# HGRN heads' four projections as two pairs, with half of the weight sums made by adding DMAs, and small work moved between engines

## The chip, the cores and the metric

The kernel runs on one core of one Trainium2 chip. The core has five engines that run side by side, each through its own queue in a fixed order: TensorE (PE in the profile; its weight loads are PEld), VectorE (DVE), ScalarE (ACT), GpSimd (POOL), and SyncE (SP), which here issues almost all DMAs. The metric is the time of one execution on the device in microseconds; lower is better. The traces are profiled executions of the same program.

## The reference

One inference step of a one-layer encoder over T = 32 + 512 tokens: 32 frames of a running stream (the sample) and 512 frames of a new one (the prompt). Everything is float32. After an RMS norm, one large projection `xn @ w_in` (1024 inputs) is cut into the parts of two branches and two gates:

```python
u, v_m, z_m, ig_pre, fg_pre, q_h, f_h, i_h, g_h, ga, gb = jnp.split(proj, _split_points(), axis=-1)
...
lfh = jnp.log(lb + (1.0 - lb) * jax.nn.sigmoid(f_lin))
kh = (1.0 - lb) * jax.nn.sigmoid(-f_lin)
qh = jax.nn.silu(q_h.astype(f32))
oh, S_new = _hgrn(to_heads(qh), to_heads(kh), to_heads(i_h.astype(f32)), to_heads(lfh), S0[l].astype(f32))
oh = _head_rmsnorm(oh.transpose(0, 2, 1, 3), hnorm_g[l].astype(f32)) * jax.nn.silu(g_h.astype(f32))
yb = oh.astype(x.dtype) @ w_brh[l]
y = jax.nn.sigmoid(ga) * ya + jax.nn.sigmoid(gb) * yb
```

The first branch is an mLSTM with four heads of 512 (its output, through `w_brm`, is `ya`). The second, HGRN2, has eight heads of 128: for each head and token, `o = q exp(g) S + sum over earlier tokens of (q, k, decay) v`, with a decay per channel, and the state `S` is carried on. Then come the gated sum, `w_out`, a small per-layer embedding behind a sigmoid gate, and the final norm. Outputs are the tokens and all new states of both streams.

## The kernel before, in words

Tokens lie along the free dimension, channels on the 128 partitions. To keep float32 accuracy, TensorE multiplies in a reduced format: each operand is split in a high part (a cast on ScalarE) and a low part (a subtraction on VectorE), and each product is three matmuls, high by high, high by low and low by high. A projection of 128 output channels is a *unit*; its weights come as two raw pieces of 128 x 512 by a DMA on SP (`raw_piece`, L118) and are split by `split_piece` (high L128, low L129).

There are two ways to make units. `One` (matmuls L366) computes one unit as eight input blocks x three products x two token halves = 48 matmuls. `Two` computes two units with seven instead of eight half-size products (Winograd's form of Strassen's method): the token sums are made once (`xf`), the weight sums s1 to s4 in `make` (VectorE, L418), each of seven blocks is 12 matmuls of 272 columns (L453), and `after1` to `after7` evict the partial products: some are kept in SBUF by ScalarE (L467), some added to or subtracted from a kept one by VectorE (L474, L476), one is negated by ScalarE (L478). With w = [[a0, a1], [b0, b1]] for units a and b and their two pieces, s1 = b0 + b1, s2 = s1 + a0, s3 = a0 + b0 and s4 = s2 + a1.

`Pump` puts the blocks of a list of units in one order (two neighbouring pairs overlap in it), loads raw pieces up to four ahead (RAWAHEAD), prepares weights three blocks ahead (AHEAD), and hands out the matmuls in steps of six. A chain of other work is a generator: each `yield n` lets the pump run n steps, and then the chain issues its own matmuls. TensorE's order is therefore written out by hand; on the other engines a scheduler fixes an order when the program is built, and SP and GpSimd too run theirs in that order. A semaphore wait holds everything behind it on its engine.

Stages: the opening (norm, first projections, gate rows); four mLSTM heads, each with a pump; then one pump for `units()`: per HGRN head h the single units f, q, i, g, and after them eight pairs of the two merge gates ga and gb. Beside that pump runs `chain(h)` for one HGRN head after another: seven levels of decay (chunk lengths 1 to 64). In each level ScalarE copies the far keys (km, L1390), TensorE makes the products pl (L1398; the sample's at L1406), VectorE multiplies keys hk and queries hq by the decay (L1416), multiplies decays with each other (L1420) and picks the level's entries into `at` under a mask (L1421, sample L1423). After the first level the diagonal terms q*k are transposed (pd) and summed (dg). Then the triangles `aa` are cut out of `at` on GpSimd with the constant `tri` (L1446, L1452), values and keys are transposed (ht), state products are made (su, L1474), the chunk states follow one from the other in VectorE (tile tf, L1477, L1479), and the outputs (ho, L1497 to L1501) read `aa`, `at` and the chunk states. The diagonal is added (L1506, L1507), and the norm follows (L1512 to L1522). `finish(h)` transposes the head's output two or three levels into the next head's chain and multiplies it by the gate.

The pump also evicts the single units of a head: `forget` makes tf and hk (sigmoids on ScalarE, scaling on VectorE, L1324 to L1329), `query` makes q, hq and kq (L1335 to L1340, kq on GpSimd), `value` copies, `gate` makes silu as x * sigmoid(x). After the chains come the rest of the gate pairs, then `w_brh`, `w_out` and the last gate.

In the opening, four value units are projected; the copy of the fourth out of PSUM (`values_out`, L1222) is called in the part where only TensorE's order is written by hand. PSUM tiles of projections share four banks (pool `pd`).

Of the kernel before, what the change touches and what calls it, by code (L numbers as in the profile page):

```python
# [14 lines left out]
ALU = mybir.AluOpType  # L15

P = 128
# [24 lines left out]
NSUM = 4  # L42
# [20 lines left out]
def hybrid_step(ctx: ExitStack, tc: tile.TileContext, a, o):  # L63
# [228 lines left out]
    tri = cp.tile([P, 2, P], F32, name="tri")  # L292
    pick(tri[:, 0, :], ALU.is_gt, 0, 1, -1, 1.0, 0.0)
    pick(tri[:, 1, :], ALU.is_gt, 0, -1, 1, 1.0, 0.0)
    sxt = cp.tile([P, P], F32, name="sxt")
# [32 lines left out]
    xf = [None] * (KD // 2)  # L328

    class One:  # L330
# [9 lines left out]
        def blocks(self, first):  # L340

            return [
                (i, [(self.unit, i // 2)] if i % 2 == 0 else [], self.prepare(i // 2) if i % 2 == 0 else None, self.run(i), {})
                for i in range(3)
            ] + [(3, [], None, self.run(3), {self.key: 1})]

        length = 4
# [35 lines left out]
    class Two:  # L383
# [3 lines left out]
        length = 7  # L387

        def __init__(self, what, f, unit, dest, then):
            self.what, self.f, self.unit, self.dest, self.then = what, f, unit, dest, then  # L390
            self.sums, self.w, self.t, self.late = {}, {}, {}, None

        def raws(self):
            a, b = self.unit, self.unit + 1
            return [(a, 0), (b, 0), (b, 1), (a, 1)]

        def blocks(self, first):
            a, b = self.unit, self.unit + 1
            times = (0, 3, 1, 6, 5, 9, 11) if first else (0, 3, 5, 6, 8, 9, 11)
            k = (self.what, self.f), (self.what, self.f + 1)  # L400
            return [
                (times[0], [(a, 0)], self.make("a11"), self.run("a11", 0, True, self.after1), {}),
                (times[1], [(b, 0), (b, 1)], self.make("s2"), self.run("s2", 0, False, self.after6), {}),
                (times[2], [(a, 1)], self.make("a12"), self.run("a12", 1, True, self.after2), {}),
                (times[3], [], self.make("s3"), self.run("s3", 0, False, self.after7), {}),
                (times[4], [], self.make("s1"), self.run("s1", 1, True, self.after5), {}),
# [3 lines left out]

        def make(self, form):
            def go(raw):
                a, b = self.unit, self.unit + 1
                q = self.sums

                def add(name, x, y):
# [1326 lines left out]
```

## Time and profile before

| | |
|---|---|
| median of 3 runs | 1174.36 us (1173.25 to 1174.53) |
| the profiled execution | 1174.53 us, its span 1172.8 us |
| busy: TensorE / VectorE / ScalarE / GpSimd | 1160.9 / 883.9 / 614.9 / 143.5 us |
| granted TensorE clock | 0.999 |
| DMA | 135.82 MB, mean 116 GB/s |
| DMA queues | SP's and ScalarE's hardware queues; no DMA is issued from GpSimd |
| one HGRN head (752.68 to 788.34 us) | 35.66 us |

Times are in us from the span's start unless marked ns. In a row of instruction groups stand line, engine, operation, output <- input with shapes, the count, then busy us and mean ns of one, and last the engine's idle time just before them and what ended it. A row of a stretch gives the busy time (and count) of PE, PEld, DVE, ACT and POOL, the granted clock, the share of the DMA engines and GB/s. A row of the chain of waits is the start, the length and the piece that the end of the program waited for. Matmuls overlap, so a row's mean is longer than the step from one to the next.

### The profile page before, as it was taken

What the parts mean: (1) busy time and instruction counts of PE and PEld (TensorE: products, weight loads), DVE (VectorE), ACT (ScalarE), POOL (GpSimd) and SP (SyncE); (2) the same over time, 40 slices, a digit from 0 to 9 for tenths busy, and PEclk for the clock granted to TensorE, in tenths of its full rate; (3) what the DMA queues carried; (4) which work ended last, traced back from release to release, by engine and by line L of the source; (5) the groups of instructions that cost most, each with busy time, mean ns of one, the idle gap of its engine ahead of it and who ended that gap; (6) DMA issues with size and microseconds to landing.
All of it is one profiled execution on the core that took longest, in us unless ns stands there. A gap on an engine that the chain in (4) does not pass through costs nothing.

```text
span 1172.8 us, 24295 instructions
## 1 busy us (share of the span) xinstructions
PE 1160.9 (99%) x9089; PEld 1130.5 (96%) x9089; DVE 883.9 (75%) x2156; ACT 614.9 (52%) x1357; POOL 143.5 (12%) x283
## 2 busy tenths in 40 slices
PE   9999999999999999999999999999999999999998
PEld 8989999999999999999999999999999999999998
DVE  6977988686996768967885677877788998654485
ACT  5676557654665556665572343343434666433462
POOL 4933011110111000210000101111101100000000
PEclk9999999999999999999999999999999999999999
DMA  6124215232353233542637222212122273332753
GB/s 231 63 94 128 91 46 175 93 109 100 122 179 115 82 118 117 173 138 93 219 102 238 64 70 62 70 62 71 55 70 63 76 242 99 106 100 77 236 170 113
DMA packets 77902, 135.82 MB, mean 116 GB/s; under 512 B 8788, under 2 KB 16340, under 8 KB 77784
## 3 DMA queue, kind: packets, MB, share of 16 engines
q1 hardware_dynamic: 77616, 134.21, 35.4%
q8 instruction: 71, 1.16, 0.4%
q14 instruction: 47, 0.39, 0.1%
q10 hardware_dynamic: 168, 0.06, 0.0%
HBM read 109.32 MB, written 24.91 MB: 114 GB/s over the span
## 4 chain that ended last, share of the span: by engine, by line
PE 86%; DVE 3%; ACT 1%; issue 1%; ACTq 0%; DVEq 0%
PE d L453 22%; PE d L366 18%; PE ya L149 8%; PE pg L1602 4%; PE yb L149 4%; PE o L149 4%; PE C L833 4%; PE q L149 3%; PE k L149 3%; PE pl L1398 2%; PE nm L1003 2%; PE sc L793 2%; PE ple L149 1%; PE nm L980 1%; PE ht L1464 1%
## 5 line engine op out<-in xcount | busy, mean ns | idle before, releaser
L1390 ACT COPY km<-hk 128x256 f32<-128x256 f32 x56 | 24.0, 429 | 82.0 <-DVE hk L1416 60.0
L569 DVE SCALAR_TENSOR_TENSOR cv<-ub,vec,cv 128x547 f32<-128x547 f32 x48 | 40.3, 840 | 1.3 <-ACT cv L564 0.7
L1398 PE MATMUL pl<-hq,km 128*128 128x128 f32 x224 | 36.0, 284 | 0.0
L1416 DVE TENSOR_TENSOR hq<-hq,q 128x128 f32<-128x128 f32 (+1 forms) x96 | 25.3, 293 | 9.5 <-PE pl L1398 8.3
L933 DVE SCALAR_TENSOR_TENSOR c<-c,wi,Cs 128x258 f32<-128x258 f32 x32 | 15.3, 477 | 21.8 <-PE Cs L931 21.8
L1398 PEld LDWEIGHTS pl<-hq,km 128*128 128x128 f32 x224 | 30.8, 190 | 0.0
L467 ACT COPY t<-d 128x272 f32<-128x272 f32 x78 | 29.6, 379 | 1.2 <-PE d L453 1.0
L1452 POOL TENSOR_TENSOR at<-at,tri 32x32 f32<-32x32 f32 x8 | 4.0, 496 | 208.5 <-DVE at L1423 208.5
L1071 DVE TENSOR_TENSOR y<-ya,y 128x272 f32<-128x272 f32 x48 | 18.9, 434 | 10.7 <-PE ya L149 10.1
L1416 DVE TENSOR_TENSOR hk<-hk,q 128x128 f32<-128x128 f32 x96 | 26.1, 285 | 0.3 <-ACT km L1390 0.2
L845 ACT COPY Co<-C 128x258 f32<-128x258 f32 x32 | 10.4, 378 | 29.2 <-PE C L833 24.7
L1421 DVE COPY_PREDICATED at<-lmask,pl 128x256 f32<-128x256 uint8 x56 | 24.7, 441 | 0.0
L1512 ACT ACTIVATE osq<-kq 128x128 f32<-128x128 f32 x32 | 9.9, 311 | 25.8 <-DVE kq L1506 25.1
L1340 POOL TENSOR_TENSOR kq<-q,hk 128x544 f32<-128x544 f32 x8 | 13.9, 1742 | 61.3 <-DVE q L1338 58.4
L1014 ACT COPY y<-nm 128x516 f32<-128x516 f32 x16 | 9.4, 590 | 21.7 <-PE nm L1003 21.7
L562 POOL COPY uo<-ub 128x3 f32<-128x3 f32 x16 | 11.5, 717 | 71.2 <-DVE ub L474 50.0
L833 PE MATMUL C<-vh,kwl 128*128 128x258 f32 x96 | 19.4, 283 | 0.0
L833 PE MATMUL C<-vl,kwh 128*128 128x258 f32 x96 | 19.4, 283 | 0.0
L833 PE MATMUL C<-vh,kwh 128*128 128x258 f32 x96 | 19.4, 283 | 0.0
L963 DVE BATCH_NORM_STATS2 bs<-y 128x6 f32<-128x512 f32 (+1 forms) x20 | 13.8, 691 | 6.4 <-ACT y L1014 6.2
L731 POOL COPY vsm<-vt 128x96 f32<-128x96 f32 x16 | 7.0, 446 | 87.1 <-ACT vt L478 44.0
L807 ACT CAST sh<-dm 128x512 fp32r<-128x512 f32 (+3 forms) x16 | 7.4, 460 | 18.9 <-DVE dm L801 17.4
(4086 smaller groups left out, 4880.1 us busy)
## 6 DMA issues: line engine op xcount, KB each, us to landing
ya_d<-y SPq DMA_DIRECT2D x32, 272.0 KB, 2.1
y<-ya_d SPq DMA_DIRECT2D x24, 272.0 KB, 4.3
c<-in_C SPq DMA_DIRECT2D x16, 258.0 KB, 3.5
out_Cp<-Co SPq DMA_DIRECT2D x16, 258.0 KB, 2.6
out_Cs<-c SPq DMA_DIRECT2D x16, 258.0 KB, 2.3
x<-in_xT SPq DMA_DIRECT2D x8, 272.5 KB, 4.8
ya<-ya_d SPq DMA_DIRECT2D x8, 272.0 KB, 4.3
h<-in_xT SPq DMA_DIRECT2D x8, 272.0 KB, 3.7
```

The lines of the kernel that those rows point to most:

```text
L149: PE.matmul(both[b][:m, :TH], part(w, off + k * step, m, x), xx[:, half(b)], start=(k == 0 and j == 0), stop=(k == n - 1 and j == 2),)
L366: PE.matmul(self.ps[b][:, : c.stop - c.start], part(self.w, k * P, P, x), xx[:, c], start=(k == 0 and j == 0), stop=(k == KD - 1 and j == 2),)
L453: PE.matmul(ps, ww[:, c], xx, start=(start and k == 0 and j == 0), stop=end, skip_group_check=not start,)
L467: S.copy(t, ps)
L569: V.scalar_tensor_tensor(cv[:, :547], ub[:, j : j + 547], vcol(V_CW + 4 * ft + j), cv[:, :547], ALU.mult, ALU.add)
L793: PE.matmul(pn[:, 0, :n], ks[f][x][:, j * P : (j + 1) * P], qs[f][y][:, NS + j * P : T], start=(f == 0 and i == 0), stop=(f == KH - 1 and ...
L833: PE.matmul(pn[g][:, :VH], kw[b][x][:, f * P : (f + 1) * P], vv[b][y][:, g * VH : (g + 1) * VH], start=(b == 0 and j == 0), stop=(b == NB ...
L1390: S.copy(km.rearrange("p (n j c) -> p n j c", j=2, c=c), view(kk, HB, ((2 * c, NA // (2 * c)), (c - HB, 2), (1, c))),)
L1398: PE.matmul(pn[:, 0, b * P : (b + 1) * P], km[:, b * P : (b + 1) * P], view(qq, b * P, ((2 * c, P // (2 * c)), (HB + c, 2), (1, c))), star ...
L1416: V.tensor_tensor(xv[:, :, i, :], xv[:, :, i, :], t[:, :, 1 - i : 2 - i].to_broadcast([P, m, c]), ALU.mult)
L1421: V.copy_predicated(at[:, :NA], lmask[:, li, :NA], pn[:, 0, :NA])
L1602: PE.matmul(ps, part(w, k * P, P, x), xx[:, c], start=(k == 0 and j == 0), stop=(k == KD - 1 and j == 2))
```

## The change

Projections of an HGRN head become two pairs: units q and f, and units g and i. `One` remains for four z units of the first mLSTM head. Per pair, the sums s1 and s3 come from DMAs: SP loads b0 into two buffers, and a DMA issued on GpSimd's queue adds b1 to the one and a0 to the other while it loads them; s2 and s4 stay on VectorE. The raw piece b0 is no longer loaded by itself. The pump begins these three blocks ahead of the pair's first block in the order of preparation (LEAD). The eight pairs of the merge gates do the same. s4 is now added in place in the buffer of s2, and the ring of sum buffers has five instead of four.

```diff
-NSUM = 4
+NSUM = 5
+LEAD = 3
...
+        def begin(self):
+            a, b = self.unit, self.other
+            for name, u, i in (("s1", b, 1), ("s3", a, 0)):
+                t = self.sum_tile(name)
+                nc.sync.dma_start(t, w_in[b][:, :WP])
+                G.dma_start(t, w_in[u][:, i * WP : (i + 1) * WP], accum_op=ALU.add)
...
                 if form == "s2":
-                    add("s1", raw[b, 0], raw[b, 1])
-                    add("s2", q["s1"], raw[a, 0])
-                if form == "s3":
-                    add("s3", raw[a, 0], raw[b, 0])
+                    if not self.early:
+                        add(self.sum_tile("s1"), raw[b, 0], raw[b, 1])
+                    add(self.sum_tile("s2"), q["s1"], raw[a, 0])
+                if form == "s3" and not self.early:
+                    add(self.sum_tile("s3"), raw[a, 0], raw[b, 0])
...
+                while self.begins and self.begins[0][0] <= self.made:
+                    self.begins.pop(0)[1].begin()
```

The eviction follows: a pair's results land in SBUF tiles (the value unit through reversed slices, `value_tile`), and ScalarE and VectorE work from there. The scalings of tf and hk move to ScalarE, silu is one ScalarE operation (so silu and sigmoid alternate there), and kq moves from GpSimd to VectorE:

```diff
-            V.tensor_scalar(tf[:, :T], tf[:, :T], lcc, lbc, ALU.mult, ALU.add)
-            V.tensor_scalar(kk[:, :T], kk[:, :T], lcc, None, ALU.mult)
+            S.activation(tf[:, :T], tf[:, :T], AF.Identity, scale=lcc, bias=lbc)
+            S.mul(kk[:, :T], kk[:, :T], lcc)
...
-            V.tensor_tensor(unrev(q0), acc[0][:, :HB], unrev(q0), ALU.mult)
-            V.tensor_tensor(q0[:, HB:T], acc[1][:, :NA], q0[:, HB:T], ALU.mult)
+            S.activation(unrev(q0), qq[:, :HB], AF.Silu)
+            S.activation(q0[:, HB:T], qq[:, HB:T], AF.Silu)
             V.tensor_tensor(qq[:, :T], q0[:, :T], tf[:, :T], ALU.mult)
-            G.tensor_tensor(kq[:, :T], q0[:, :T], kk[:, :T], ALU.mult)
+            V.tensor_tensor(kq[:, :T], q0[:, :T], kk[:, :T], ALU.mult)
```

In the chain the sample's product gets 128 instead of 32 weight columns, so one mask operation serves both parts, and one operation multiplies both sides' decays from the second level on; the diagonal sums come from one reduction; the triangles are cut by GpSimd's select without the constant `tri`; the diagonal terms are made by ScalarE ahead of the outputs, which VectorE then adds; one state copy and the norm's last products move to ScalarE; `finish` comes one level later.

```diff
-                PE.matmul(pn[:NS, 0, NA:HB], kk[:, csmp], qq[:, csmp], start=True, stop=True)
+                PE.matmul(pn[:, 0, NA:HB], kk[:, NA : NA + P], qq[:, csmp], start=True, stop=True)
...
-            V.copy_predicated(at[:, :NA], lmask[:, li, :NA], pn[:, 0, :NA])
-            if smp:
-                V.copy_predicated(at[:NS, NA:HB], lmask[:NS, li, NA:HB], pn[:NS, 0, NA:HB])
+            V.copy_predicated(at[:, :n], lmask[:, li, :n], pn[:, 0, :n])
...
-            if li == 2 and h:
+            if li == 3 and h:
...
-            G.tensor_tensor(
-                aa[:, j],
-                at[:, :NA].rearrange("p (b t) -> p b t", b=2),
-                tri[:, j : j + 1, :].to_broadcast([P, 2, P]),
-                ALU.mult,
-            )
+            for b in range(2):
+                triangle(aa[:, j, b], at[:, b * P : (b + 1) * P], 1 - 2 * j)
...
+                for b in range(NB):
+                    S.mul(ov[:, b * P : (b + 1) * P], it[:, b * P : (b + 1) * P], dg[:, b : b + 1])
...
-        V.tensor_copy(sb[:, :P], pu[:, 0, :P])
+        S.copy(sb[:, :P], pu[:, 0, :P])
...
-            V.scalar_tensor_tensor(ov[:, d], it[:, d], dg[:, b : b + 1], po[:, 0, d], ALU.mult, ALU.add)
+        V.tensor_tensor(ov[:, :NP], po[:, 0, :], ov[:, :NP], ALU.add)
...
+        for b in range(NB):
+            S.mul(ov[:, b * P : (b + 1) * P], ov[:, b * P : (b + 1) * P], hr[:, b : b + 1])
```

Two smaller moves: the new sample state `sn` shares its two buffers with the loaded one (`s0`), and the mask input `sxt` a buffer of the small pool. In the opening, the last `values_out()` is called ahead of the gate rows, in the part where ScalarE's order too is written by hand:

```diff
         st8[0]["wk"] = weight(a["w_km"][0, 0], "wk00", eng=G)
+        values_out()
         for _ in range(GATED):
             next(gates)
```

209 lines of the change are left out of this document (116 added, 93 removed).

## Prediction

> **What bounds the kernel now.** I read first the page's busy times and the shares of the chain that ended last, then the busy times by stage, then the chain of waits inside one HGRN head, and last the rows of VectorE, ScalarE, GpSimd and the DMA queue there. The page, its head and a line of its fourth part:
>
> ```profile
> span 1172.8 us, 24295 instructions
> ...
> PE 1160.9 (99%) x9089; PEld 1130.5 (96%) x9089; DVE 883.9 (75%) x2156; ACT 614.9 (52%) x1357; POOL 143.5 (12%) x283
> ...
> PE d L453 22%; PE d L366 18%; PE ya L149 8%; PE pg L1602 4%; PE yb L149 4%; PE o L149 4%; PE C L833 4%; PE q L149 3%; PE k L149 3%; PE pl L1398 2%; PE nm L1003 2%; PE sc L793 2%; PE ple L149 1%; PE nm L980 1%; PE ht L1464 1%
> ```
>
> TensorE sets the time, and the single projections (L366) and the paired ones (L453) are its largest parts. By stage, one window in which the last head runs beside paired projections, and one whole head beside single ones (columns: engine busy us, TensorE clock, DMA share, GB/s):
>
> ```profile
> 894.00:927.00 33.00, 32.97 (x253) 30.60 (x253) 31.09 (x89) 14.79 (x34) 3.25 (x3) 1.00 0.14 43
> 752.68:788.34 35.66, 35.66 (x279) 33.71 (x279) 27.04 (x99) 14.05 (x39) 4.04 (x5) 1.00 0.21 65
> ```
>
> A head takes 35.66 us and TensorE has no gap in it; VectorE is busy 27.04 us and ScalarE 14.05 us. The chain of waits through that head, and the longest piece of paired projections after the heads:
>
> ```profile
> 773.03 0.45 PE pl L1398 x4
> ...
> 780.57 0.44 PE ho L1497 x4
> ...
> 781.91 0.22 PE ho L1499 x2
> ...
> 788.17 0.18 PE pl L1406 x2
> ...
> 939.02 54.37 PE d L453 x431
> ```
>
> Every link is TensorE. A 272-column matmul costs 54.37/431 = 0.126 us at the margin. Two times matter below, counted from the last level's product at 773.03: the outputs (ho) come 7.5 us later, and the last read of a chunk state 8.9 us.
>
> **The change, part by part.**
>
> *Pairs instead of singles.* Two single projections are 2 x 48 = 96 matmuls, a pair 7 x 12 = 84. Sixteen pairs remove 192 matmuls: 192 x 0.126 = 24.2 us, all on the path. The other insertions of a head stay, so its pitch would fall by 3.0 us to 32.6 us. 28 pump steps a head now equal the 28 that a chain consumes (27 without the finish), so chain follows chain; work after the last head shrinks from 92 to 84 steps of 6 matmuls.
>
> *Wider sample weights.* The 40 sample products now load 128 weight columns instead of 32. Two passes took 0.18 us, and four 128-wide ones 0.45 us, thus 0.09 against 0.11 each: 0 to 40 x 0.04 = 1.6 us. I take 0.8.
>
> *VectorE.* Rows of the head, and of the window after it where they exist only there:
>
> ```profile
> L1339 DVE TENSOR_TENSOR hq<-q,tf 128x544 f32<-128x544 f32 x1 | 1.9, 1897 | 0.0
> L1420 DVE TENSOR_TENSOR q<-q 128x4 f32<-128x4 f32 (+9 forms) x12 | 1.5, 177 | 0.0
> L1506 DVE SCALAR_TENSOR_TENSOR kq<-hi,dg,ho 128x128 f32<-128x128 f32 x4 | 1.1, 340 | 0.0
> L1423 DVE COPY_PREDICATED at<-lmask,pl 32x32 f32<-32x32 uint8 x5 | 0.9, 173 | 0.0
> L1354 DVE TENSOR_TENSOR hg<-d,hg 128x272 f32<-128x272 f32 x2 | 0.8, 432 | 0.0
> L1516 DVE TENSOR_TENSOR kq<-kq,hr 128x512 f32<-128x512 f32 x1 | 0.7, 692 | 0.0
> L129 DVE TENSOR_TENSOR wi760l<-wi76r,wi760h 128x512 fp32r<-128x512 f32 x1 | 0.7, 692 | 1.7 <-ACT wi760h L128 1.7
> L1328 DVE TENSOR_SCALAR tf<-tf,lc,lb 128x544 f32<-128x544 f32 x1 | 0.6, 559 | 0.0
> L1329 DVE TENSOR_SCALAR hk<-hk,lc 128x544 f32<-128x544 f32 x1 | 0.5, 499 | 0.0
> L1337 DVE TENSOR_TENSOR q<-d,q 128x288 f32<-128x288 f32 x1 | 0.5, 458 | 2.1 <-ACT q L1335 2.1
> L1338 DVE TENSOR_TENSOR q<-d,q 128x256 f32<-128x256 f32 x1 | 0.4, 414 | 0.0
> ```
> ```profile
> L1361 DVE TENSOR_TENSOR ya<-ya,ga 128x544 f32<-128x544 f32 x2 | 1.4, 725 | 0.0
> L418 DVE TENSOR_TENSOR ws<-ws,wi88r 128x512 f32<-128x512 f32 x2 | 1.4, 688 | 0.0
> ```
>
> Added to a head: 6 more low parts (14 pieces instead of 8) x 0.69 = 4.2; the sums s2 and s4 of two pairs, 4 x 0.69 = 2.8; 6 evictions x 0.43 (the 272-wide row, L1354) = 2.6; kq from GpSimd 0.7: 10.3 us. Removed: the scalings of tf and kk 1.1; the two products with q 0.9; of the gate 0.9; hq falls from 1.9 to about 0.7, since kq no longer runs beside it on GpSimd, 1.2; the output norms 0.7 and their small sample part about 0.3; four diagonal terms and a sample one become two adds, 0.7; the sample masks join the wide ones, 0.7 net; six of the short products of the decay 6 x 0.18 = 1.1; a state copy about 0.3: 7.9 us. VectorE ends at 27.04 + 2.4 = 29.4 us of 32.7, 90%. The first window shows 31.09 of 33.00 us (94%) with TensorE at 32.97 in just such a mix, so I take nothing for load alone. In the branch gates two sums a pair leave VectorE; TensorE is the limit there, and I take nothing.
>
> *ScalarE.* Rows of the head, the page's row of the kept products, and two of the opening:
>
> ```profile
> L128 ACT CAST wi760h<-wi76r 128x512 fp32r<-128x512 f32 x1 | 0.6, 618 | 1.4 <-PE d L366 1.4
> L1512 ACT ACTIVATE osq<-kq 128x128 f32<-128x128 f32 x4 | 1.2, 311 | 2.9 <-DVE kq L1506 2.8
> ```
> ```profile
> L467 ACT COPY t<-d 128x272 f32<-128x272 f32 x78 | 29.6, 379 | 1.2 <-PE d L453 1.0
> ```
> ```profile
> 70.67 1.28 ACT L641 ACT_TABLE_LOAD   x1
> 71.96 0.66 ACT L641 ACTIVATE row<-row 4x544 f32<-4x544 f32 x1
> ```
>
> Added: 6 high parts 3.7; 6 kept and 2 flipped products x 0.38 = 3.0; two 544-wide scalings x 0.66 = 1.3; ten 128-wide products for diagonal and norm x 0.31 = 3.1; a state copy 0.3; two table loads, since silu and sigmoid now alternate, 2 x 1.28 = 2.6. Removed: the value copies and one half of the gate's, 0.9. ScalarE goes to 14.05 + 13.1 = 27.2 us of 32.7, 83%. Its lead of three blocks (three pump blocks are 4.5 us of matmuls) covers the casts; if that cover is gone, a late copy km is late for the next level's product. Page against trace: the Trainium skill, "ScalarE: Activation LUTs", What ACT_TABLE_LOAD costs, adds a drain and puts each switch at about 2.66 us; by that, an estimate, ScalarE would be at 30.0 us and its rival below more likely. The trace does not agree: the activation starts at 71.96, when the 1.28 us are over.
>
> *The adding DMAs.* Per pair two plain loads go to SP's queue and two accumulating ones to GpSimd's; one raw load falls away. Each accumulating one waits on GpSimd for its plain load. Four a head stand in one queue with the triangles and the clearing of at. Rows of the load, of its issue, and of GpSimd:
>
> ```profile
> wi69r<-in_w_in SPq DMA_DIRECT2D x2, 256.0 KB, 2.6
> ```
> ```profile
> 777.96 0.33 SPq L118 DMA_DIRECT2D wi62r<-in_w_in  x1
> ```
> ```profile
> 774.44 1.45 POOL L1446 TENSOR_TENSOR aa<-at,tri 128x256 f32<-128x256 f32 x2 [3.60 <-DVE at L1421]
> L175 POOL TENSOR_SCALAR_AFFINE_SELECT tri<-tri x2: 293/536/778, 3.5 to 4.9; 128x128 f32<-128x128 f32 x2
> ```
>
> In the built order of the changed kernel, in each head, the first accumulating DMA of the next g/i pair stands on GpSimd just ahead of the four triangles, and VectorE's sum s2, which reads its result, stands ahead of the update of the third chunk state. The plain load waits for a buffer that VectorE frees with a low part which I place 0.7 us after the last level's product, behind the products hq and kq. Three issues x 0.4 = 1.2, landing 2.6: 4.5 us after the product. Triangles then take 4 x 0.3 = 1.2 us and are ready before 7.5 unless GpSimd spends over 1.8 us on the DMA. The accumulation from GpSimd's turn to landing is not in the trace: at least the 2.6 us of a plain load, at most about twice that and a GpSimd operation of 1.4 us, 6.6. I take 4.0, nearer to the plain load. Then 4.5 + 4.0 + 0.7 (s2) + 0.3 (update, at the nearest 128-wide row, L1506) = 9.5 against 8.9 us: TensorE waits 0.6 us a head, 8 x 0.6 = 5 us. Bounds: 0 and 8 x 3.2 = 26 us. On SP's queue the next head's sample state now waits, buffers being shared, for ho of the head before, with raw loads behind it; they are issued four pieces ahead of need, more than a pair's 7 blocks of 1.5 us, and I take nothing.
>
> *The opening.* The fourth value copy moves ahead of the gate rows:
>
> ```profile
> 72.94 0.67 PE L149 MATMUL k<-cs0h,wk000h 128*128 128x272 f32 x2 [2.37 <-ACT vt L1222]
> 75.52 0.69 ACT L603 ACTIVATE z<-d 128x272 f32<-128x272 f32 x2
> ```
>
> The wait of 2.37 us ends, but the second k product (due 3 us after the first, at 75.9) needs the banks that z frees at 76.2. ScalarE has the same work ahead of z in either order. The wait moves there: I take 0.3 us of 0 to 2.4.
>
> **Sum**, against the profiled execution of 1174.53 us (span 1172.8 and 1.7 around it; the median of the runs is 1174.36, 0.2 less): 1174.5 - 24.2 + 0.8 - 0.3 + 5 = 1155.8 us.
>
> **Rivals.**
> 1. VectorE or ScalarE becomes the bound of a head through its fixed order. Before, VectorE idles 35.66 - 27.04 = 8.6 us a head; if half of that stays, the pitch is 29.4 + 4.3 = 33.7, or 1.0 us a head over 32.7; with three quarters 3.1. For it: ScalarE doubles. Against it: the 94% window. 8 x 1.0 in place of the 5: 1158.8; at 2 us a head 1167.
> 2. Slower: the accumulation lands late. Each us beyond 3.4 us from GpSimd's turn goes straight into the wait at ho. 24.2 + 0.3 - 0.8 = 23.7 us over 8 heads is 3.0 us a head, so it decides from 6.4 us; at 8 us it is 4.6 x 8 = 37: 1174.5 - 23.7 + 37 = 1187.6. For it: no such DMA is in the trace, and GpSimd and VectorE held each other up (hq 1.90 us beside kq, 0.73 for the same shape elsewhere). Against it: only this one sum of the four a head has so little lead; that of the next q/f pair is read some fifty VectorE instructions after its buffer comes free.
> 3. About the same: VectorE holds up GpSimd while it writes such a DMA's descriptors. Held by one operation of hq's 1.9 us, the landing is 4.0 + 1.9 = 5.9 us, the wait 2.5 us a head or 20 us: 1174.5 - 23.7 + 20 = 1170.8; a second hold on the triangles would close the rest. For it: hq beside kq. Against it: the scalings L1328 and L1329 leave the head. The Trainium skill, "SBUF — State Buffer", SBUF: two separate sides, speaks against the change: descriptors of GpSimd's DMAs cannot be written while VectorE runs a two-port operation, and 0.62 us became 3.1 us there. By that rule this rival is the likely one; hq's row agrees that the two engines block each other, and no run so far has such a DMA.
> That the matmuls do not go is excluded by the built order: 192 fewer.
>
> **How the numbers follow.** Forecast with waits under 1 us a head 0.62 (own range 1148 to 1161); rival 1 0.18 (1159 to 1170); rival 2 0.14; rival 3 0.06, half of it within 0.2% of the time before. No change from no wait at all is 1174.5 - 24.2 - 2.4 = 1148. The range 1147 to 1170 holds the first two. About 0.2% (2.3 us) is what a measurement can tell: faster 0.81, same 0.04, slower 0.15, the last with a little of rival 1's far end.
>
> **What would show it.** Right: pitch between first levels near 33.3 us; paired projections at 0.126 us; a wait at ho of about 0.6 us named for the state tile tf; 30 and 27 us busy on VectorE and ScalarE a head; a software DMA queue whose transfers land 4 us after issue; an early wait that now precedes the second k product. Wrong: TensorE waits at pl for km or hq (rival 1), at ho for aa (GpSimd's queue held the triangles), or for weights of a sum (rival 2), or transfers of more than 6 us.

## The result, and the profile after

The changed kernel takes 1179.01 us (median of 4 runs, 1178.62 to 1181.02), the kernel before 1174.34 us beside it (1173.25 to 1174.53). The ratio is 1.0048, with a 95% interval of 1.0035 to 1.0060: slower by about half a per cent, where 1155.8 us and 1147 to 1170 had been forecast. The profiled execution took 1178.68 us.

The page of the changed kernel, its head, the busy times and the chain that ended last:

```profile
span 1176.7 us, 24263 instructions
PE 1140.0 (97%) x8897; PEld 1110.7 (94%) x8897; DVE 891.7 (76%) x2092; ACT 708.9 (60%) x1565; POOL 181.6 (15%) x335
PE 17%; ACT 1%; DVE 0%; issue 0%; ACTq 0%
```

TensorE has 192 instructions fewer and is busy 20.9 us less, but the span is 3.9 us longer. The chain's 17% for TensorE, after 86% before, says little of where the time went: followed back from the end, it reaches only to 965.50 us, in the merge gates' pairs, and says nothing of the time before. TensorE's waits tell more. Each row names what waited, what ended the wait, and then the us in total, the times and the longest:

```profile
PE pl L1446 <- ACT km L1438: 8.5, 9, 1.1
PE d L467 <- DVE hq L488: 5.3, 1, 5.3
PE d L467 <- ACT t L481: 3.0, 2, 2.1
PE ht L1510 <- DVE hq L1464: 2.6, 6, 0.4
PE k L151 <- ACT z L635: 2.2, 1, 2.2
PE ya L151 <- DVE y L1103: 1.6, 4, 0.4
PE ya L151 <- ACT wbm301h L130: 1.2, 1, 1.2
```

Of these only the wait before k has a counterpart before (2.37 us). The others stand in four places.

**In the heads.** One head after, by the busy times of a stretch (PE, PEld, VectorE, ScalarE, GpSimd, clock, DMA share, GB/s):

```profile
740.78:774.75 33.97, 32.41 (x254) 30.98 (x254) 29.41 (x92) 25.60 (x66) 7.54 (x10) 1.00 0.47 115
```

The pitch fell from 35.66 to 33.97 us. VectorE is busy 29.41 us (29.4 forecast) and ScalarE 25.60 (27.2). No engine is full, and TensorE still waits, twice in most heads. The timeline at the first wait (in brackets the engine's idle time before the row and what ended it):

```profile
738.86 1.28 ACT L1564 ACTIVATE kq<-kq,hr 128x128 f32<-128x128 f32 x4
...
740.34 0.39 ACT L1438 COPY km<-hk 128x256 f32<-128x256 f32 x1
740.78 0.71 PE L1446 MATMUL pl<-hq,km 128*128 128x128 f32 x4 [1.13 <-ACT km L1438]
```

The five norm multiplications that the change moved to ScalarE (four in the first row, the sample's left out here) run back to back just ahead of the copy km, and TensorE stands 1.13 us until that copy is done. The same row comes back every 34 us, seven times. Some 12.5 us later, in six heads, the second transposes (ht) wait 0.4 us for the last level's hq.

**At the first pair of head 0**, where the fourth mLSTM head ends:

```profile
607.34 0.72 DVE L104 TENSOR_TENSOR hm15l<-c,hm15h 128x544 fp32r<-128x544 f32 x1
607.97 0.43 DVE L488 TENSOR_TENSOR hq<-d,t 128x272 f32<-128x272 f32 x1
608.46 0.59 PE L467 MATMUL d<-xfh,ws148h 128*128 128x272 f32 x1 [5.29 <-DVE hq L488]
608.85 0.43 PE L467 MATMUL d<-xfl,ws148h 128*128 128x272 f32 x1
609.08 0.43 PE L467 MATMUL d<-xfh,ws148l 128*128 128x272 f32 x1
...
614.00 0.29 PE L467 MATMUL d<-xh,wa1172h 128*128 128x272 f32 x1
614.12 0.29 PE L467 MATMUL d<-xl,wa1172h 128*128 128x272 f32 x1
```

The fifth block of a pair starts anew in the PSUM bank of the third, so VectorE must first evict the third's result into hq. In VectorE's order that eviction stands behind the last chunk of the branch (hm15). TensorE is idle 5.29 us, and then 24 matmuls step by 0.227 us (608.85 to 609.08) instead of 0.125 (614.00 to 614.12), another 2.4 us. The clock shows why (busy us, granted clock, DMA share, GB/s):

```profile
608.00:610.00 2.00, 1.54 (x7) 0.50 0.67 213
614.00:616.00 2.00, 2.00 (x18) 1.00 0.74 201
```

**At the last branch products** (ya, 619 to 651 us) a product starts every 4.00 and 3.82 us by turns, 3.91 on average (624.64 to 648.08 us), with waits of 0.41 and 0.50 us. Before, it was every 3.00 us without a wait. First the kernel before, then the changed one:

```profile
616.95 0.41 PE L149 MATMUL ya<-hm12h,wbm300h 128*128 128x272 f32 x2
619.95 0.41 PE L149 MATMUL ya<-hm12h,wbm310h 128*128 128x272 f32 x2
```
```profile
624.64 0.74 PE L151 MATMUL ya<-hm12h,wbm300h 128*128 128x272 f32 x2 [0.41 <-DVE y L1103]
628.64 0.65 PE L151 MATMUL ya<-hm12h,wbm310h 128*128 128x272 f32 x2 [0.50 <-ACT wbm311h L130]
```

A stop costs about twice what the wait in its row shows, 0.91 against 0.46 us on average: the ends of matmuls are modelled in the profile, and the first two after a stop take 0.74 or 0.65 us here, not the 0.41 of before.

**In the gate pairs**, from 957 to 976 us, waits of 2.07, 0.89 and 1.02 us. The first of them:

```profile
953.15 0.33 SPq L404 DMA_DIRECT2D ws<-in_w_in  x1
953.53 0.43 SPq L1599 DMA_DIRECT2D p<-in_pT  x1
958.28 0.64 ACT L103 CAST ps0h<-p 128x544 fp32r<-128x544 f32 x1 [4.16 <-DMA p<-in_pT]
...
959.39 0.36 ACT L481 COPY t<-d 128x272 f32<-128x272 f32 x1
959.81 0.39 PE L467 MATMUL d<-xfh,ws384h 128*128 128x272 f32 x1 [2.07 <-ACT t L481]
```

On SP the load of p stands behind a new plain load of a sum, which had waited 3.4 us for one of the five sum buffers. On ScalarE the cast of p stands ahead of the kept product t, and TensorE needs t to go on. Three queues in a row pass one wait on.

### The profile page after: what moved, and what is told of

It is laid out like the page before. It is cut to its first block, busy times and chain, and to the rows that moved or that the text cites. A ratio compares the mean times of both kernels' runs of the same rounds, so it can differ in the third digit from the quotient of the medians.

```text
span 1176.7 us, 24263 instructions
## 1 busy us (share of the span) xinstructions
PE 1140.0 (97%) x8897; PEld 1110.7 (94%) x8897; DVE 891.7 (76%) x2092; ACT 708.9 (60%) x1565; POOL 181.6 (15%) x335
## 5 line engine op out<-in xcount | busy, mean ns | idle before, releaser
L405 POOL DMA_DIRECT2D ws<-in_w_in x48 | 42.1, 877 | 301.8 <-DMA ws<-in_w_in 57.4
L481 ACT COPY t<-d 128x272 f32<-128x272 f32 x126 | 47.5, 377 | 2.7 <-PE d L467 2.2
L1473 DVE COPY_PREDICATED at<-lmask,pl 128x288 f32<-128x288 uint8 (+1 forms) x56 | 26.3, 469 | 0.0
L1421 POOL TENSOR_SCALAR_AFFINE_SELECT aa<-at 128x128 f32<-128x128 f32 x32 | 25.5, 829 | 2.3 <-DVE at L1473 2.3
L1464 DVE TENSOR_TENSOR hk<-hk,q 128x144 f32<-128x144 f32 (+1 forms) x96 | 25.1, 290 | 0.7
L593 POOL COPY uo<-ub 128x3 f32<-128x3 f32 x16 | 17.5, 1092 | 39.0 <-DVE ub L490 28.8
```

Source lines behind the costliest of these rows:

```text
L405: G.dma_start(t, w_in[u][:, i * WP : (i + 1) * WP], accum_op=ALU.add)
L481: S.copy(t, ps)
L1421: G.affine_select(out=out, in_=x, compare_op=ALU.is_gt, fill=0.0, base=0, pattern=[[-sign, n]], channel_multiplier=sign)
L1464: V.tensor_tensor(xv[:, :, i, :], xv[:, :, i, :], t[:, :, 1 - i : 2 - i].to_broadcast([P, m, c]), ALU.mult)
L1473: V.copy_predicated(at[:, :n], lmask[:, li, :n], pn[:, 0, :n])
```

## The experiments

Times are medians beside runs of the kernel before (1174.3 to 1174.6 us). The ratio to it stands in brackets with its 95% interval. "The changed kernel" is 1179.0 us.

### Norm multiplications back on VectorE

```diff
-        for b in range(NB):
-            S.mul(ov[:, b * P : (b + 1) * P], ov[:, b * P : (b + 1) * P], hr[:, b : b + 1])
-        S.mul(osb, osb, hr[:NS, NB : NB + 1])
+        V.tensor_tensor(
...
+            hr[:, :NB].rearrange("p (b o) -> p b o", o=1).to_broadcast([P, NB, P]),
+            ALU.mult,
+        )
+        V.tensor_scalar(osb, osb, hr[:NS, NB : NB + 1], None, ALU.mult)
```

> One part undone: the four norm multiplications of a head and the one of its sample go back from ScalarE to VectorE in the form of the kernel before. Theory (ScalarE's order): the copy of the next head's keys for its first level stands behind these multiplications (738.86 to 740.34 us in one head of the changed kernel), and TensorE waits 1.13 us for it in each of seven heads (8.5 us in all in pl). Undone, these waits go: about 1179 - 7 = 1171 to 1173 us. Rival (VectorE is as full as ScalarE): the 0.7 us a head that VectorE gets back turns up as a wait for hq or for a put, and the gain is under 3 us: 1176 to 1180.

Measured: 1170.94 us (0.9975, 0.9966 to 0.9983). The waits in pl are gone but for one of 0.41 us, and a head is:

```profile
752.62:785.18 32.56, 32.14 (x255) 30.93 (x255) 30.09 (x96) 24.21 (x61) 8.10 (x11) 1.00 0.53 120
```

The theory held: this single part of the change cost 8.1 us. Undone, the pitch is 32.56 us, with VectorE busier than in the changed kernel.

### Only ScalarE's order changed

Two edits were to leave the multiplications on ScalarE. The first issued them one level later, in the run with four edits (below); the order on ScalarE came out as it had been, so it told nothing of the order:

```diff
+            if li == 1 and h:
+                scaled(h - 1)
```

> As the run with four edits, but the norm multiplications stay on ScalarE and are issued one level later in the next head, behind the copy that waited for them. Theory (order, not the sum of ScalarE's work): within 2 us of that run, 1156 to 1160. Rival (ScalarE's 27 us of 33 a head are the matter): the waits in pl stay at some 1 us a head at another level, 1163 to 1168.

Measured: 1169.04 us (0.9959, 0.9946 to 0.9971), with the 1.13 us in pl in every head as before. It isolates the norm in another way, though: beside the run with four edits, whose other three edits are the same, ScalarE's norms cost 8.6 us (1169.0 against 1160.4).

The second gave the copy km priority, which puts it ahead of the multiplications:

```diff
-            S.copy(
-                km.rearrange("p (n j c) -> p n j c", j=2, c=c),
...
+            with tc.high_priority():
+                S.copy(
+                    km.rearrange("p (n j c) -> p n j c", j=2, c=c),
```

> The changed kernel, and only the order of ScalarE is changed: the copy of a level's keys goes ahead of the five norm multiplications (and of other work that is ready with it), which stay on ScalarE. The run that issued them one level later had left that order as it was. Theory (order, not ScalarE's load): the waits of 1.13 us go as with the multiplications on VectorE, 1170 to 1173. Rival (ScalarE's sum of work): the five multiplications delay the next cast of weights by the same 1.5 us and TensorE waits there, 1176 to 1180.

Measured: 1174.49 us (0.9996, 0.9987 to 1.0005), between the two. The waits in pl are gone. In their place the second transposes wait longer, 0.83 to 1.07 us in each of seven heads, for ScalarE's copies of the first ones. TensorE's row, and ScalarE's ahead of it:

```profile
753.45 0.66 PE L1511 MATMUL ht<-ident,hk 128*128 128x128 f32 x4 [0.83 <-ACT kit L1514]
```
```profile
750.92 0.39 ACT L481 COPY t<-d 128x272 f32<-128x272 f32 x1 [0.21 <-PE d L467]
...
751.72 0.53 ACT L1439 COPY km<-hk 128x256 f32<-128x256 f32 x1
752.15 0.62 ACT L130 CAST wa2275h<-wi67r 128x512 fp32r<-128x512 f32 x1
...
753.15 0.25 ACT L1514 COPY kit<-ht 32x128 f32<-32x128 f32 x1
```

So the order explains the wait at that place, and 3.5 us of the 8.1 stay. A head takes 32.95 us (740.61 to 773.56 us) against 32.56 with the norms on VectorE, which is most of it. The multiplications themselves, at 740.3 us, no longer hold these copies up: at 750.92 us ScalarE has caught up and waits 0.21 us for TensorE. What stands ahead of the copies is casts and the next head's first copy km, which the priority has moved there.

### The moves alone, and the pairs with most moves undone

```diff
-            yield Two(
...
+            yield One(("f", h), 56 + h, HB, lambda acc, h=h: forget(h, acc))
+            yield One(("q", h), 48 + h, HB, lambda acc, h=h: query(h, acc))
+            yield One(("i", h), 64 + h, HB, lambda acc, h=h: value(h, acc))
+            yield One(("g", h), 72 + h, TH, lambda acc, h=h: gate(h, acc))
```

> The moves between the engines without the pairs: the heads' four projections are single units as before the change (48 matmuls each), and the gate pairs have all sums on VectorE; triangles, norms, diagonal, gate functions and products stay where the change put them. Theory (the moved work costs only because the pairs took away the products that covered it): a head has 35.7 us of matmuls, the multiplications ahead of the copy for pl find them, and the time stays within 3 us of the kernel before, 1172 to 1177. Rival (the moves cost by themselves): the wait of 1.13 us in pl stands in seven heads here too, 1180 to 1184.

Measured: 1184.61 us (1.0083, 1.0068 to 1.0097). My theory fell: TensorE waits without the pairs too, 1.76 us in most heads, at another copy, behind the forget gate's functions:

```profile
730.31 1.28 ACT L1358 ACT_TABLE_LOAD   x1
...
732.73 0.86 ACT L1360 ACTIVATE tf<-tf,lb,lc 128x544 f32<-128x544 f32 x1
733.46 0.76 ACT L1361 ACTIVATE hk<-hk,lc 128x544 f32<-128x544 f32 x1
734.10 0.42 ACT L1425 COPY km<-hk 128x256 f32<-128x256 f32 x1
734.57 0.60 PE L1433 MATMUL pl<-hq,km 128*128 128x128 f32 x3 [1.76 <-ACT km L1425]
```

The burst is a table load, four sigmoids and the two scalings that the change had moved, 3.8 us in one piece. ScalarE is busy only 21.1 of 36.96 us there. The same kernel with the copy km first:

> The run with the moves alone (single units, 1184.6 us), with the copy of the keys ahead of the forget gate's functions on ScalarE. Theory (the moves cost through ScalarE's order, pairs or no pairs): the seven waits of 1.76 us go, 12 us: 1172 to 1176, the time of the kernel before. Rival (the moved work is too much for ScalarE): 1179 to 1185.

Measured: 1168.27 us (0.9943, 0.9931 to 0.9956). All seven waits go, and the moves alone make the kernel 6 us faster than before, beyond what either theory gave. A head takes 34.92 us without a wait of TensorE, 0.74 less than before:

```profile
742.87:777.79 34.92, 34.92 (x280) 33.92 (x279) 22.44 (x76) 20.92 (x55) 1.58 (x6) 1.00 0.22 67
```

Most of these 6 us is the sample product, below.

The other half: pairs and adding DMAs stay, while norms, diagonal, scalings and first state copy go back to VectorE and kq to GpSimd.

```diff
-            S.activation(tf[:, :T], tf[:, :T], AF.Identity, scale=lcc, bias=lbc)
-            S.mul(kk[:, :T], kk[:, :T], lcc)
+            V.tensor_scalar(tf[:, :T], tf[:, :T], lcc, lbc, ALU.mult, ALU.add)
+            V.tensor_scalar(kk[:, :T], kk[:, :T], lcc, None, ALU.mult)
...
-            V.tensor_tensor(kq[:, :T], q0[:, :T], kk[:, :T], ALU.mult)
+            G.tensor_tensor(kq[:, :T], q0[:, :T], kk[:, :T], ALU.mult)
...
-        V.tensor_tensor(ov[:, :NP], po[:, 0, :], ov[:, :NP], ALU.add)
+            V.scalar_tensor_tensor(ov[:, d], it[:, d], dg[:, b : b + 1], po[:, 0, d], ALU.mult, ALU.add)
...
-        S.copy(sb[:, :P], pu[:, 0, :P])
+        V.tensor_copy(sb[:, :P], pu[:, 0, :P])
```

> The pairs and the adding DMAs stay; of the moves, the norm multiplications, the diagonal, the scaling of the forget gate and the first chunk state go back to VectorE and the product of keys and queries to GpSimd (Silu and the triangles stay moved). By rows of the changed kernel and the one before VectorE gets about 2.3 us a head more than the 29.4 us it has in 33.97 us. Theory (VectorE has room for it up to 32.6 us, ScalarE's order is what costs): 1168 to 1173, as the run with the norm multiplications alone. Rival (VectorE at 97% sets the pitch): waits for hq, hk or a put grow, 1175 to 1185.

Measured: 1186.37 us (1.0101, 1.0086 to 1.0116); the rival, and 1.4 us beyond its range. A head takes 35.5 us, VectorE is busy 31.8 of them (90%), and TensorE waits for VectorE's products:

```profile
PE pl L1446 <- DVE q L1472: 8.4, 5, 1.7
```

So the pairs need some of the moves: 31.8 us would be 98% of a pitch of 32.56 us, and VectorE's fixed order does not reach that.

### The start: PSUM banks and open pairs

```diff
+                if form == "s1" and self.third:
+                    self.ps = [self.ps[0], pd.tile([P, 512], F32, tag="h", name=f"d{self.unit}c")]
...
-                base += length
+                base += length + (3 if isinstance(e, Two) and e.third else 0)
```

> The first pair of head 0 starts its second product of the upper half in a PSUM buffer of its own, and the pair behind it begins three places later. Theory (a buffer that waits for its put): TensorE's 5.29 us before that product, and the half clock in the 5 us behind them (24 products at 0.227 in place of 0.126 us, 2.4 us), go: 1171 to 1173. Rival (all of VectorE is late there, because the branch's chunks stand ahead): TensorE stands still at the next place that needs VectorE, and at most 3 us are gained: 1176 to 1179.

Measured: 1177.50 us (1.0030, 1.0018 to 1.0042); the rival's range, and the 1.5 us gained are not clear of the noise (the changed kernel's interval begins at 1.0035). The 5.29 us are gone, and TensorE stands 6.00 us a little later, at the branch's first weights, again followed by half the clock:

```profile
618.46 0.82 PE L151 MATMUL ya<-hm12h,wbm300h 128*128 128x272 f32 x2 [6.00 <-ACT wbm300h L130]
```
```profile
620.00:622.00 2.00, 2.00 (x9) 0.50 0.56 146
```

On ScalarE that cast stands behind head 0's gate functions and two table loads (609.96 to 617.8 us). It is ScalarE that is full there, not VectorE as the rival had it: VectorE waits for ScalarE's casts, 1.99 and 1.22 us before its rows at 612.50 and 615.36 us. The 12 us of products ahead of the branch are too little cover.

Finishing more pairs ahead of the branch:

```diff
-        pump.to(8 * LASTBR)
+        pump.to(14 * LASTBR)
```

> One number changed: both pairs of head 0 are finished ahead of the last branch products (28 steps in place of 16), so no pair stands half done and holds two of the four PSUM buffers while the branch's products run. Theory (PSUM): the waits of 0.41 and 0.50 us that come by turns before the branch's products (seven, 3.2 us), which the kernel before does not have, go; with the 0.44 and 1.16 us at their start about 4 us: 1174 to 1176. Rival (ScalarE's casts of the branch's weights or VectorE's adds are late by themselves): the waits stay, 1178 to 1180.

Measured: 1179.58 us (1.0046, 1.0033 to 1.0058): no gain, the waits at ya stay. But the edit missed its aim: neighbouring pairs overlap, so after 28 steps a pair was open all the same. The second attempt also starts head 1's pair later:

```diff
-                base += length
+                base += length + (5 if e.unit == 72 else 0)
...
-        pump.to(8 * LASTBR)
+        pump.to(14 * LASTBR)
```

> The run with 28 steps ahead of the branch didn't close the pairs: the first block of head 1's pair stands ahead of the last ones of head 0's second pair, so a pair was open all the same. Here the third pair begins five places later, and after 28 steps no pair is open. Theory (PSUM buffers held by an open pair): the seven waits of 0.41 and 0.50 us before the branch's products go, about 3.2 us: 1175 to 1177. Rival (the casts and adds of that stage are late by themselves): the waits stay, 1178 to 1180.

Measured: 1174.99 us (1.0009, 1.0000 to 1.0018), 4.0 us less than the changed kernel. The waits of 0.41 and 0.50 us are all gone, and a product starts every 3.00 us again. With the same 28 steps and an open pair they had stayed, so the cause is shown: a half-finished pair holds two of the four PSUM banks, and the branch's products, which need two each, can no longer overlap their evictions. Before, 16 steps were just two complete single units. The 5.29 us at the first pair stay.

### The adding DMAs

```diff
-                True,
+                False,
...
-            yield pair("ga", f, 80 + f, lambda f: plain(eslot(f"ga{f}")), merge_a, True)
-            yield pair("gb", f, 88 + f, lambda f: plain(eslot(f"gb{f}")), merge_b, True)
+            yield pair("ga", f, 80 + f, lambda f: plain(eslot(f"ga{f}")), merge_a)
+            yield pair("gb", f, 88 + f, lambda f: plain(eslot(f"gb{f}")), merge_b)
```

> One part undone: all four sums of the pairs of heads and gates are made by VectorE again, and no adding DMA is left. Theory (the adding DMAs are not what costs): no wait of TensorE in the changed kernel ends with one of them; without them VectorE has 2 x 0.69 us a pair more, 2.8 us a head on 30 of 34 us, and the time grows by 2 to 10 us: 1181 to 1189. Rival (the transfers hold up VectorE or the weights): the time falls by 3 us or more, to 1176 or less.

Measured: 1176.44 us (1.0018, 1.0009 to 1.0027), 2.6 us less than the changed kernel: neither theory's figure. The heads keep their pitch with VectorE at 31.8 us a head; the waits in the gate pairs are gone. Only the gate pairs' DMAs undone (the two lines of ga and gb):

> The pairs of the heads keep their adding DMAs; the pairs of the branch gates have all their sums on VectorE, as before the change. The kernel with all sums on VectorE took 1176.4 us in place of 1179.0, and the trace of that run has no wait of TensorE between 920 and 1000 us, where the changed kernel has three, 2.07, 0.89 and 1.02 us. Theory (the adding DMAs of the gate pairs cost these 4 us, those of the heads nothing and bring nothing): 1174.5 to 1176.5, no wait of TensorE in the gate pairs. Rival (the 2.6 us came from the heads): 1178 to 1180, waits of the gate stage as in the changed kernel.

Measured: 1176.21 us (1.0016, 1.0007 to 1.0024), with no wait of TensorE between 914 and 999 us. p is loaded at 949.81 us, 3.7 us earlier, and its cast is done at 954.6. The whole gain came from the gates, as the theory had it.

### Four edits together

Norms on VectorE, gate sums on VectorE, the third bank, and no open pair at the branch (the third pair five places later); all four diffs stand above.

> Four edits together: norm multiplications on VectorE as before the change, sums of the gate pairs on VectorE, the third PSUM buffer for head 0's first pair, and no pair open at the branch. Theory (the matmuls taken out are worth what was reckoned, 24 us, and the loss sits in these four places): 1179 less 8.1 (measured), 4.0 of the gate stage, 3.2 at the branch's products, and 5 to 7.7 at the first pair (with 21 us of products in place of 12 ahead of the branch, ScalarE's 7 us for the first head's gates are covered): 1156 to 1160. Rival (VectorE and ScalarE at 85 to 90% set the pitch, each place given back moves the wait to the next): 1162 to 1170.

Measured: 1160.44 us (0.9895, 0.9880 to 0.9910), 18.6 us less than the changed kernel, 0.4 us above what the theory gave. Alone the edits gave 8.1, 2.8, 1.5 and 4.0, a sum of 16.4 us. The difference of 2.2 us is about what the intervals allow; that the third bank gains more once 21 us of products stand ahead of the branch is possible, but no run separates it. The sums of the heads put on VectorE too:

> As the run with four edits, and the sums of the heads' pairs on VectorE too, so that no adding DMA is left. A head of that run has VectorE busy 30.07 of 32.56 us; two pairs with two sums of 0.69 us more make 32.8. Theory (here, with the pitch down to the products, the adding DMAs are worth something): the pitch becomes VectorE's, 33 us or more, 1164 to 1170. Rival (the adding DMAs are worth nothing at all): 1159 to 1162.

Measured: 1166.32 us (0.9932, 0.9919 to 0.9944), as the theory had it. Here the adding DMAs of the heads are worth 5.9 us: a head takes 34.5 us with VectorE at 32.3, and TensorE waits for it twice a head. Under the waits of the changed kernel that worth had not shown.

With kq back on GpSimd (one line, as in the run with the moves undone):

> As the run with four edits (1160.4 us), and the product of queries and keys goes back to GpSimd. Theory (the 0.4 us before the second transposes of a head come from VectorE, which has the two products of the next head's query, 0.72 us each, ahead of the last level's): six waits of 0.4 us go, 1157 to 1159. Rival (GpSimd's 1.7 us delays the next adding DMA, triangles, or the diagonal's transposes): no gain or 1161 to 1166.

Measured: 1163.57 us (0.9912, 0.9898 to 0.9925), 3 us more by the medians; the intervals overlap, but the rows go the same way. A head takes 33.03 us (746.05 to 779.08 us), not 32.56, and the 0.4 us before the second transposes became 0.9, because VectorE's hq takes 1.89 us beside GpSimd's kq. In the run with four edits, where both products are VectorE's, it takes 0.72. First this run, then that one:

```profile
775.85 1.70 POOL L1373 TENSOR_TENSOR kq<-q,hk 128x544 f32<-128x544 f32 x1 [2.82 <-ACT q L1371]
776.24 1.89 DVE L1372 TENSOR_TENSOR hq<-q,tf 128x544 f32<-128x544 f32 x1
```
```profile
774.48 0.72 DVE L1372 TENSOR_TENSOR hq<-q,tf 128x544 f32<-128x544 f32 x1
```

Three more orders of ScalarE. Copy km first, norms on ScalarE, the other three edits as they were:

> The pairs closed and the third buffer at head 0, gate sums on VectorE, and the copy of the keys first, with the norm multiplications left on ScalarE, so that VectorE keeps its 29.4 us a head. Theory (order): the time of the run with these four places and the norms on VectorE, 1160.4 us, or up to 2 us less, 1158 to 1161. Rival (ScalarE's load): 1163 to 1169.

Measured: 1162.02 us (0.9892, 0.9878 to 0.9905); the wait of 0.83 us before the second transposes stands in six heads again, 1.09 in the first. Against the run with the norms one level later (1169.0 us, 0.9946 to 0.9971) that is 7 us from ScalarE's order alone. The copies of the transposes first as well:

```diff
-            S.copy(dst, pt[:, 0, :])
-            S.copy(dss, pt[:NS, 1, :P])
+            with tc.high_priority():
+                S.copy(dst, pt[:, 0, :])
+                S.copy(dss, pt[:NS, 1, :P])
```

> The same order on ScalarE with the norm multiplications left there, as in the run of 1162.0 us, whose waits were the 0.83 us before the second transposes behind the diagonal's multiplications. Theory (order): these seven waits go, 6 us: 1155 to 1158. Rival (ScalarE's work, put off, is late for the weights instead): 1160 to 1165.

> The run with four edits (1160.4 us, norm multiplications on VectorE), and on ScalarE the copies of a level's keys and those of the transposes go ahead of the diagonal's multiplications. Theory (order): the six waits of 0.4 us before the second transposes go, 1156 to 1159. Rival (VectorE at 30.1 of 32.6 us sets those waits): 1160 to 1163.

Measured: 1160.69 us with the norms on ScalarE (0.9889, 0.9874 to 0.9903), 1159.78 us with the norms on VectorE (0.9877, 0.9864 to 0.9891). Neither theory held: waits of 0.3 to 0.6 us stay. The copies had not stood behind the diagonal's multiplications, as both expectations had it, but behind casts and a copy km, as in the rows above. These two, the run before them and the run with four edits are the same within their intervals. Once ScalarE's order is right, it hardly matters which engine has the norms.

### The wide sample product on the kernel before

```diff
-                PE.matmul(pn[:NS, 0, NA:HB], kk[:, csmp], qq[:, csmp], start=True, stop=True)
+                PE.matmul(pn[:, 0, NA:HB], kk[:, NA : NA + P], qq[:, csmp], start=True, stop=True)
```

> The kernel before with one edit of the change: the 40 products of the sample's keys and queries take 128 columns of weights in place of 32. Theory (from rows of two kernels: from the first pl product of a level to the next weight product pass 0.76 us before and 0.62 us with the wide product, 5 levels a head, 8 heads): 5.6 us less, 1168 to 1170, where the prediction had 0.8 us more. Rival (the 0.14 us come from the other moves): 1174 to 1176.

Measured: 1170.25 us (0.9967, 0.9954 to 0.9979). Loading 128 weight columns instead of 32 saves 4.2 us. The same level before, and with the edit alone:

```profile
756.28 0.64 PE L1398 MATMUL pl<-hq,km 128*128 128x128 f32 x4
756.86 0.25 PE L1406 MATMUL pl<-hq,hk 128*32 128x32 f32 x2
757.03 0.52 PE L366 MATMUL d<-xh,wi751h 128*128 128x272 f32 x2
```
```profile
754.73 0.64 PE L1398 MATMUL pl<-hq,km 128*128 128x128 f32 x4
755.22 0.30 PE L1406 MATMUL pl<-hq,hk 128*128 128x32 f32 x2
755.35 0.50 PE L366 MATMUL d<-xh,wi751h 128*128 128x272 f32 x2
```

From the first product of the level to the next projection: 0.75 us before, 0.62 with the wide product.

## Why the prediction was wrong

| term of the sum | forecast | what the runs showed |
|---|---|---|
| 192 matmuls | -24.2 | -22: they are gone. A head without waits: 34.92 us with single units (moves, copy first), 32.56 - 0.42 with pairs: -2.8 a head |
| wide sample product | +0.8 | -4.2 |
| opening | -0.3 | the wait is 2.16 instead of 2.37 us |
| wait at ho for the chunk state | +5 | 0: no wait at ho |
| norms in ScalarE's order | 0 | +8.1 |
| open pair at the branch | 0 | +4.0 |
| adding DMAs in the gate pairs | 0 | +2.8 |
| first pair's PSUM bank | 0 | 5.3 us of wait and 2.4 of half clock; 1.5 by itself, since the wait moves on |

**The step that failed** is the one from load to cover: work that was moved or stood at a seam was costed at nothing because the engine had time left. For ScalarE the prediction added up the busy time (83%) and took nothing. It named the copy km and said it would be late if the cover went, but the sum has no term for it. The load was right, VectorE to 0.1 us and ScalarE high by 1.6. The time was lost to the order within the load: five multiplications of 0.3 us that become ready together stand in front of the copy that TensorE needs next. The 94% window was no evidence against that, since VectorE was the full engine in it (ScalarE 14.79 of 33.00 us) and the burst is not in it.

**Rival 1** named this kind of loss, and its sign to look for, a wait at pl for km, is what the trace shows; the price of 1 to 2 us a head fits (1.13 and 0.43 in waits). But it was priced by VectorE's idle time, and it got 0.18.

**The second failure** is that the sum ended at the heads. Where stages meet, a pair needs an eviction between two of its blocks, which a single unit does not, and it holds its banks longer. "TensorE is the limit there, and I take nothing" was the sentence for the gate pairs. The wait there came through SP, where the new plain loads stand ahead of the load of p. The pitch of 32.6 us was to be had, as the run with the norms back shows, though that 32.56 agrees so well is partly luck: the matmuls gave 2.8 us a head, not 3.0, the wide product some 0.5 that had not been forecast, and a wait of 0.42 us is in it. The four places together cost 18.6 us, and without them the kernel comes to 1160.4 us, 4.6 us over the forecast. That is near by luck too: the 5 us at ho were not paid and the wide product saved 4.2 us, and some 10 us of other waits made up for both.

**The wide product** was priced by the lengths of rows, 0.09 against 0.11 us a pass, and came out with the wrong sign. Matmuls overlap: what counts is the step to the next projection, 0.75 against 0.62 us.

**The adding DMAs** were priced nearly right and placed wrong. They land 4.4 us after issue (3.8 to 6.3; 4.0 taken). But the one ahead of the triangles was issued 1.5 us after the last level's product, not 4.5: its plain load had gone out at 749.21 us, ahead of that product, and by its row it waited for VectorE's kq. In the head whose last level begins at 751.00 us:

```profile
752.49 0.91 POOL L405 DMA_DIRECT2D ws<-in_w_in  x1 [4.87 <-DVE kq L1370]
753.77 3.49 POOL L1421 TENSOR_SCALAR_AFFINE_SELECT aa<-at 128x128 f32<-128x128 f32 x4 [0.37 <-DVE at L1473]
759.21 0.61 PE L1548 MATMUL ho<-hi,aa 128*128 128x128 f32 x4
```

The four triangles took 3.5 us, not the 1.2 reckoned, and were still in time. Rivals 2 and 3 did not occur: ScalarE, which casts these sums, never waited for such a DMA, and VectorE only twice, 1.97 us in the first head (662.85 us) and 0.79 us in the gate pairs (943.24 us), and TensorE has no wait at ho. The Trainium skill, "SBUF — State Buffer", SBUF: two separate sides, has the descriptors of GpSimd's DMAs wait while VectorE runs a two-port operation, which lent rival 3 its rule. It could still hold for single transfers, the slowest of which took 6.3 us, but no run here shows it; at a median of 4.4 us it set nothing.

What of the 1179.0 us is left unexplained: without waits the terms give 1174.5 - 22 - 4.2 = 1148 us. The four edits return 18.6 us, and the run with them still has some 10 us of new waits in its rows, most of them between 609 and 631 us and before the second transposes. That leaves 2 us, about what stops may cost beyond their rows; where they lie is open.

## What to carry to other kernels

Load is not cover: where queues run in a fixed order, list for each engine the instructions on which the bounding engine waits, and ask which moved burst can stand in front of each of them. When a unit of work needs an eviction between its parts, count the PSUM banks it holds at each seam with the next stage, and check what the seam's other user needs. And undo parts one by one: here a gain of some 26 us (the pairs and the wide product) was present all along under 31 us of waits and of what follows them, and four small edits brought 1179.0 down to 1160.4 us.

## What the runs showed of the hardware

- **A narrow weight load costs time around it.** Loads of 32 columns take 108 ns and of 128 columns 192 ns by their rows, and yet the level with the narrow one takes 0.13 us longer, 4.2 us in the 40 products (1170.25 against 1174.44 us). The Trainium skill, "TensorE: Matmul & The Clock Gate", Step-by-step: what each phase is for, says that a weight load's time scales with its columns. The loads' own rows agree in direction, but the time of the sequence does not follow them. Why, these runs do not show.
- **The clock halves after shorter stops than expected.** After 5.29 and 6.00 us of idle TensorE the granted clock was 0.50 for 5 us and more, and in the run with only the copy km first from 956 to 960 us too, after 3.21 us. The kernel before also shows 0.52 to 0.62 from 74 to 78 us, behind its wait of 2.37 us. Behind waits of 2.07 and 2.16 us the changed kernel kept 1.00, while with the same 2.16 us before k the run with four edits fell to 0.50. The Trainium skill, "TensorE: Matmul & The Clock Gate", HAM oscillation — how this bites in real kernels, warns of idle gaps over about 3.4 us; here gaps of 2.2 to 2.4 us were sometimes enough, and what decides is open.
- **A two-input product on GpSimd holds up one on VectorE**: hq takes 1.89 us beside GpSimd's kq and 0.72 us without, shown above by moving nothing but kq. Whether GpSimd's product is held up too, no run shows.
